# Dilated queries projected by seven-product block pairs together with the keys, rotated as stored halves; one weave of eight plain units over all twelve attention items

## The chip, the cores and the metric

The kernel runs on one core of a Trainium2 chip. The metric is device time in microseconds (us) of one execution; the comparison is between the median of runs of the kernel before and of the kernel after. The engines are named as in the profile: PE (matrix products), PEld (PE's weight loads), DVE, ACT and POOL (elementwise work), SP (a queue that here issues DMAs only).

## The reference

One block with three parallel mixers over 1024 tokens of width 1024, in float32. What matters here is the first mixer, the dilated window attention, and the merge gates:

```python
h = rms_norm(x, g_pre[layer])
a_qkv, bq, bk, bv, mq, ga, gb, gm, mg = jnp.split(h @ w_in[layer], split_at, axis=-1)
a_qkv = a_qkv.reshape(b, s, 3, n_groups * A_HEADS, HEAD_DIM)   # 3 groups x 8 heads x 64
aq = rope(a_qkv[:, :, 0], pos)
ak = rope(a_qkv[:, :, 1], pos)
av = a_qkv[:, :, 2]
for gi, (window, dil) in enumerate(A_GROUPS):                  # (128,1), (512,4), (2048,16)
    hs = slice(gi * A_HEADS, (gi + 1) * A_HEADS)
    o_g, lse_g = dilated_window_attention(aq[:, :, hs], ak[:, :, hs], av[:, :, hs], window, dil)
...
wts = jax.nn.softmax(jnp.stack(lses, axis=0), axis=0)          # over the three groups
oa = einsum(wts, outs)
...                                                            # grouped-query and memory attention
gates = sigmoid(mg + b_merge)                                  # 3 x 1024 columns of h @ w_in
merged = gates[0] * ya + gates[1] * yb + gates[2] * ym         # y: gated branch outputs, projected
x = x + rms_norm(merged @ w_out, g_post)
```

`rope` turns a head's first 32 features x1 and last 32 features x2 by an angle per token: x1 cos - x2 sin, and x1 sin + x2 cos.

## The kernel before

**Operands.** The normalised input is held transposed in SBUF, 8 tiles of 128 features by 1024 tokens, as a high part `hh` and a low part `hl` in a reduced format; weights are split likewise (`split`, L104: ACT copies the high part, DVE subtracts it from the source to get the low one). A product is three passes: high by high, high by low, low by high. A *unit* is 128 columns of `w_in` (1024 x 128 weights, 512 KB). A *plain* unit (`dense`, L139) takes 48 matmuls of 512 columns: 8 feature tiles, 3 passes, 2 token halves.

**Block products.** Two units can be made together by a scheme with seven products of half-sized blocks in place of eight (`PRODUCTS`: A11, A12, S2, S3, S4, S1, A22 of the weights, with sums S1 to S4 of weight blocks, against B and T blocks of the tokens, T being sums of token blocks that are kept in DRAM as `tsd`). Each product is 12 matmuls of 512 columns, a pair of units 84 instead of 96. The price is elementwise work per pair: four sums of weight blocks on POOL, splits of the blocks on ACT and DVE, and seven evacuations of PSUM with adds on DVE.

**Stages.** After the normalisation, the memory attention and the grouped-query attention come, in the order of time:

- the *value stage* (products for the dilated values);
- the *key stage* (loop at L1251): the twelve units of dilated keys as six pairs. `k_load` fetches two units, `k_sum` makes the sums on POOL, `k_own` and `k_block` split, `k_evac` takes PSUM, `k_out` adds the last part of a result and puts `turn_it` on the list `turns`: two multiplications on DVE, by the cosine table and by the sine table (`tab`, resident in SBUF), and two stores to `kd` issued from ACT's queue;
- the *weave* (from L1301 to the end of the pool `aa`): the twelve *items* of dilated attention, one for each pair of heads `p_` and group `g`, are interleaved with sixteen plain units: twelve of dilated queries (`add_a`), four of a mixer's gate (`add_ag`). `weave` (L176) places, in program order, a plain matmul or a piece of attention, whichever is behind by its planned cost. Deferred elementwise pieces lie in `pend`, and one is taken every third matmul. An item has 8 tiles of 128 queries: `scores` (PE), `soft` (a masked minimum on DVE, an exponential on ACT), `trans` (PE transposes, a copy by ACT), `pv` (PE), with `trans` three tiles behind `soft`. `combine` weighs the three groups of a head pair by their log-denominators, through DRAM, with multiplications on DVE (`weigh`, L1674) and adds on POOL;
- the *merge-gate stage* (loop at L1937): the other 22 of the 24 merge-gate units as eleven pairs of seven products, each finished by a tanh and a store to `thd`; two (`FILL_B`) are made earlier, beside the grouped-query attention;
- the branch products with the merge, and the output product.

**Queries and keys before.** A query unit's PSUM result is rotated by `q_rope`: four DVE operations of 32 partitions each for the crossed part (x2 by sine and x1 by sine, with the sign in the table), one DVE operation of 128 partitions for the straight part, and a POOL add that also writes the tokens sorted by residue class (`half_of`, `classes`). A key unit comes back from DRAM two items ahead: `k_fetch` loads `kraw` (cosine part) and, in four DMAs, `kswp` (sine part with the half heads exchanged), and `k_add` adds them on POOL, sorted by class. The first two query units and `first_keys` stand ahead of the first item, in a weave of their own; each later item has a weave of its own with one query unit, the last one the four gate units less one.

**Order.** In all these stages ACT, DVE, POOL and SP run in the order of the program (`manual_schedule`), and so does PE. An instruction that waits holds up everything behind it on its engine. Plain units of the weave: `add_au`, where `a_fetch` loads two units ahead and `a_split` splits the next unit's weights in two halves.

Of the kernel before, what the change touches and what calls it, by code (L numbers as in the profile page):

```python
# [16 lines left out]
NT = 8  # L17
# [33 lines left out]
def block(ctx: ExitStack, tc: tile.TileContext, x, xT, memT, cst, msk, bcst, tabA, gpost,  # L51
# [188 lines left out]
    kd = dram.tile([2, 12, P, S], F32, name="kd")  # L240
# [791 lines left out]
    def k_load(n, u):  # L1032

        KR[n, u] = wp.tile([P, 1024], F32, name="wr", bufs=WR)
        nc.sync.dma_start(KR[n, u], wu[4 * n + 2 * u + 1])


    AU = [2 * m for m in range(12)] + [U_G + 4 * i + p_ for i, p_ in GATES_A]
# [39 lines left out]
    kr_turn = iter(range(64))  # L1078

    def kr():  # L1080
        return vb.tile([P, 512], F32, name=("vy2", "vy3", "vv0", "vv1", "vy0", "vy1")[next(kr_turn) % 6])

    def k_out(n, u, t, ps_, z):

        r = kr()
        V.tensor_tensor(r, ps_, z, op=OP.add)

        def turn_it():
            c = kr()
            V.tensor_tensor(c, r, tab[0][:, half[t]], op=OP.mult)  # L1090
            V.tensor_tensor(r, r, tab[1][:, half[t]], op=OP.mult)
            for x, z in enumerate((c, r)):
                nc.scalar.dma_start(kd[x, 2 * n + u, :, half[t]], z)
        turns.append(turn_it)

    turns = []

    def k_evac(n, i, ps_):
        nm = PRODUCTS[i][0]
# [151 lines left out]
    for n in range(6):  # L1251
        for i, (an, bn) in enumerate(PRODUCTS):
# [11 lines left out]
            if i == 0:  # L1264
                k_block(n, "A22")
                if n < 5:
                    k_load(n + 1, 0)
            elif i == 1:
                k_block(n, "S4")
                if n < 5:  # L1270
# [6 lines left out]
            if n == 5:  # L1277
# [16 lines left out]
    close(kpp)  # L1294
    close(vbp)
# [7 lines left out]
    with tc.tile_pool(name="aa", bufs=1, reuse_waits="tile") as aa:  # L1303
# [7 lines left out]
        def half_of(ap, half, g):  # L1311

            if g == 0:
                return ap[:, half * 512:half * 512 + 512]
            n = S // DIL[g] // 2
            return ap.rearrange("p (r u) -> p r u", r=DIL[g])[:, :, half * n:half * n + n]

        def classes(ap, g):
            return ap if g == 0 else ap.rearrange("p (u r) -> p r u", r=DIL[g])

        OPS = {}

        def q_rope(o, half, p, g):

            t = slice(half * 512, half * 512 + 512)
            t1 = ab.tile([P, 512], F32, name="t1a", bufs=2)
            t2 = aa.tile([P, 512], F32, name="t2a", bufs=2)
            def cross(a):
                i, j = slice(32 * a, 32 * a + 32), slice(32 * (a ^ 1), 32 * (a ^ 1) + 32)
                V.scalar_tensor_tensor(t2[i], p[j], -0.125, tab[1][j, t], op0=OP.mult, op1=OP.mult)  # L1330

            def straight():
                V.scalar_tensor_tensor(t1, p, -0.125, tab[0][:, t], op0=OP.mult, op1=OP.mult)  # L1333
                G.tensor_tensor(half_of(o, half, g), classes(t1, g), classes(t2, g), op=OP.add)  # L1334

            pend.extend([lambda a=a: cross(a) for a in range(4)] + [straight])
# [21 lines left out]
        def add_a(p_, g):  # L1358
            d = OPS.setdefault((p_, g), {})

            def evac(half, p):
                if half == 0:
                    d["q"] = ab.tile([P, S], F32, name="aq", bufs=2)
                q_rope(d["q"], half, p, g)

            add_au(evac)

# [14 lines left out]
        KK = {}  # L1382

        def k_fetch(p_, g):

            KK[p_, g] = kr, ks = [ab.tile([P, S], F32, name=x) for x in ("kraw", "kswp")]
            nc.sync.dma_start(kr, kd[0, p_ * 3 + g])
            for a in range(4):
                i, j = slice(32 * a, 32 * a + 32), slice(32 * (a ^ 1), 32 * (a ^ 1) + 32)
                nc.sync.dma_start(ks[i], kd[1, p_ * 3 + g, j])  # L1390

        def k_add(p_, g):
            kr, ks = KK.pop((p_, g))
            ka = OPS.setdefault((p_, g), {})["k"] = ab.tile([P, S], F32, name="ak", bufs=2)
            for x in range(2):
                t = half[x]
                G.tensor_tensor(half_of(ka, x, g), classes(kr[:, t], g), classes(ks[:, t], g), op=OP.add)  # L1397

        def item(p_, g):
# [82 lines left out]
            def trans(T):  # L1482
# [25 lines left out]
                A.activation(pp[:, :k], tp[:, :k], AF.Copy)  # L1508
# [62 lines left out]
        def plan(it, pre, nxt):  # L1571
# [7 lines left out]
            def tokens(T):  # L1579
                if T >= 2:  # L1580
                    for nm, k in late[:2]:
                        split_block(nm, k)
                    del late[:2]
                if T == 5:
                    token_tiles("T1", [ab.tile([P, S], R, name=f"a{c}", bufs=2) for c in "qk"])
# [744 lines left out]
```

## Time and profile before

| what | value |
|---|---|
| median of 3 runs | 1414.22 us (1413.75 to 1416.55) |
| the profiled execution, first to last instruction (span) | 1412.1 us |
| mean granted TensorE clock | 0.999 |
| PE, DVE, ACT, POOL busy share of the span | 98%, 75%, 47%, 35% |
| key stage (580 to 692 us): PE, DVE, POOL busy | 112.0, 93.9, 32.3 us |
| weave (692 to 986 us): PE, DVE, ACT, POOL busy | 292.2, 207.4, 176.1, 108.2 us |
| merge-gate stage (986 to 1197 us): PE, DVE, POOL busy | 211.0, 171.5, 72.3 us |
| DMA | 216.01 MB, 153 GB/s over the span |

The busy time of an engine counts its instructions from start to end, with what they wait for inside an instruction. Matmuls overlap in the records, so their mean duration (some 400 ns for 512 columns) is longer than the distance of one from the next. In the lines quoted below, a timeline row is: start, duration, engine, line, operation, written tile <- read tiles, shape, count, and in brackets the idle time before it and what ended it. A group row is: line, engine, operation, tiles, shape, count | busy us, mean ns of one | idle us before it and what ended that. A row of a table by stage is: the stretch, its length, then busy us (and the number of instructions) of PE, PEld, DVE, ACT and POOL, the granted clock, DMA share and GB/s.

### The profile page before, as it was taken

The page shows a single profiled execution, that of the slowest core. Times are in us where ns is not written, and L with a number is a line of the kernel's source. Part 1 is how long each engine was busy: PE and PEld are TensorE (multiplying, and loading weights), DVE is VectorE, ACT ScalarE, POOL GpSimd, SP SyncE. Part 2 cuts the span into 40 slices and gives each one's busy share as a digit, 9 for nine tenths or more (in the row PEclk, how much of TensorE's full clock was granted, in tenths as well). Part 3 has the DMA queues.
Part 4 walks back from the last instruction along what each step waited for, and adds up shares of the span by engine and source line. Part 5 has one row for each costly group of instructions (what it writes and reads, how often), then busy time and mean ns, then how long its engine had stood idle before and what let it go on. Part 6 is the DMA issues. An engine that isn't in the chain of part 4 may idle for free.

```text
span 1412.1 us, 21576 instructions
## 1 busy us (share of the span) xinstructions
PE 1389.9 (98%) x7640; PEld 1126.2 (80%) x7640; DVE 1054.0 (75%) x1839; ACT 665.0 (47%) x1414; POOL 500.3 (35%) x390
## 2 busy tenths in 40 slices
PE   7999999999999999999999999999999999999997
PEld 7799986666666889888888878787888888888886
DVE  7768677767763688788875777765878788677977
ACT  6544365666555445222146666656443334222332
POOL 0416702666657000333153353520423331035303
PEclk9999999999999999999999999999999999999999
DMA  6356532322210787445643554555343543866255
GB/s 235 101 179 211 186 109 86 116 83 71 83 55 25 243 261 240 125 148 175 201 140 90 135 162 115 138 144 180 106 150 127 176 175 124 323 216 207 94 206 179
DMA packets 121852, 216.01 MB, mean 153 GB/s; under 512 B 25424, under 2 KB 58000, under 8 KB 121744
## 3 DMA queue, kind: packets, MB, share of 16 engines
q1 hardware_dynamic: 106096, 189.17, 42.0%
q10 hardware_dynamic: 15648, 25.47, 4.9%
q8 instruction: 60, 0.98, 0.3%
q14 instruction: 48, 0.39, 0.1%
HBM read 149.21 MB, written 65.37 MB: 152 GB/s over the span
## 4 chain that ended last, share of the span: by engine, by line
PE 88%; DVE 4%; ACT 3%; DMA 2%; POOL 2%; issue 1%; SPq 0%; DVEq 0%; ACTq 0%; POOLq 0%
PE s L125 23%; PE sc L125 9%; PE d L143 7%; PE d L147 6%; PE d L145 6%; PE s L1177 4%; PE s L2101 4%; PE ov L809 4%; PE s L1226 3%; PE tr L1522 3%; PE s L1466 3%; PE s L794 2%; PE s L793 2%; PE tr L775 2%; PE d L2101 2%; PE d L550 1%
## 5 line engine op out<-in xcount | busy, mean ns | idle before, releaser
L143 PE MATMUL d<-hh,wh 128*128 128x512 f32 x480 | 195.1, 406 | 2.4 <-DVE fth L228 2.4
L145 PE MATMUL d<-hl,wh 128*128 128x512 f32 x480 | 194.3, 405 | 0.0
L147 PE MATMUL d<-hh,wl 128*128 128x512 f32 x480 | 190.9, 398 | 0.0
L800 POOL TENSOR_TENSOR bl<-bl,bp 128x512 f32<-128x512 f32 x96 | 130.6, 1361 | 54.4 <-ACT bp L796 49.0
L105 ACT ACTIVATE wh<-wr 128x512 fp32r<-128x512 f32 (+1 forms) x93 | 72.5, 787 | 122.1 <-PE sc L125 75.3
L106 DVE TENSOR_TENSOR wl<-wr,wh 128x1024 fp32r<-128x1024 f32 (+1 forms) x67 | 85.3, 1285 | 50.2 <-ACT wh L105 50.2
L125 PE MATMUL sc<-hh,wh 128*128 128x512 f32 x384 | 118.5, 389 | 0.0
L143 PEld LDWEIGHTS d<-hh,wh 128*128 128x128 f32 x480 | 90.5, 188 | 27.8 <-issue 6.6
L147 PEld LDWEIGHTS d<-hh,wl 128*128 128x128 f32 x480 | 90.6, 189 | 21.0 <-issue 4.5
L1479 ACT ACTIVATE pra<-pra,sts 128x192 f32<-128x192 f32 (+2 forms) x192 | 84.3, 442 | 46.3 <-DVE sts L1478 45.8
L145 PEld LDWEIGHTS d<-hl,wh 128*128 128x128 f32 x480 | 90.6, 189 | 19.2 <-issue 4.5
L796 ACT ACTIVATE bp<-s 128x512 f32<-128x512 f32 x128 | 75.7, 595 | 43.3 <-PE s L794 42.3
L776 DVE TENSOR_REDUCE bn<-tr 128x1 f32<-128x512 f32 x128 | 84.9, 683 | 12.8 <-PE tr L775 11.7
L125 PEld LDWEIGHTS sc<-hh,wh 128*128 128x128 f32 x384 | 72.1, 188 | 14.9
L1330 DVE SCALAR_TENSOR_TENSOR t2a<-d,tab 32x512 f32<-32x512 f32 x96 | 65.9, 687 | 23.2 <-PE d L147 21.4
L2006 POOL TENSOR_TENSOR acc<-acc,th 128x1024 f32<-128x1024 f32 x15 | 41.4, 2757 | 109.1 <-DVE th L2005 109.1
L1789 POOL TENSOR_TENSOR sf<-wr 128x512 f32<-128x512 f32 x22 | 29.8, 1373 | 131.3 <-DVE ch L106 57.4
L125 PE MATMUL sc<-hl,wh 128*128 128x512 f32 x192 | 74.8, 389 | 0.0
L125 PE MATMUL s<-hh,ch 128*128 128x512 f32 x224 | 73.5, 390 | 0.0
L1334 POOL TENSOR_TENSOR aq<-t1a,t2a 128x512 f32<-128x512 f32 x24 | 44.6, 1861 | 72.0 <-DVE t1a L1333 72.0
L1819 ACT ACTIVATE rs<-rs,hbm 128x512 f32<-128x512 f32 x44 | 31.8, 722 | 76.5 <-DVE rs L1818 75.8
L1397 POOL TENSOR_TENSOR ak<-kraw,kswp 128x512 f32<-128x512 f32 x24 | 47.8, 2015 | 54.7 <-DMA std<-sr 21.2
(500 smaller groups left out, 3775.6 us busy)
## 6 DMA issues: line engine op xcount, KB each, us to landing
wr<-in_wu SPq DMA_DIRECT2D x64, 512.0 KB
th<-thd SPq DMA_DIRECT2D x24, 512.0 KB
thd<-rs ACTq DMA_DIRECT2D x44, 256.0 KB
kd<-vy ACTq DMA_DIRECT2D x32, 256.0 KB
g2d<-fth SPq DMA_DIRECT2D x24, 256.0 KB
wos<-os SPq DMA_DIRECT2D x12, 512.0 KB
kraw<-kd SPq DMA_DIRECT2D x12, 512.0 KB
kswp<-kd SPq DMA_DIRECT2D x48, 128.0 KB
```

The costliest lines, as they stand in the source:

```text
L105: A.activation(dst_h, src, AF.Copy)
L106: V.tensor_tensor(dst_l, src, dst_h.bitcast(F32), op=OP.subtract)
L125: PE.matmul(out_ps, a, b, start=i == 0, stop=i == n - 1)
L143: PE.matmul(dst, wh[:, k, :], hh[k][:, t], start=k == 0, stop=False)
L145: PE.matmul(dst, wh[:, k, :], hl[k][:, t], start=False, stop=False)
L147: PE.matmul(dst, wl[:, k, :], hh[k][:, t], start=False, stop=k == 7)
L776: fp["last"] = V.tensor_reduce(st[i]["n"][:, j, c:c + 1], s, axis=AX.X, op=OP.min)
L796: A.activation(pp, s, AF.Exp, scale=-1.0)
L800: G.tensor_tensor(lsum[i % 2], lsum[i % 2], pp, op=OP.add)
L1330: V.scalar_tensor_tensor(t2[i], p[j], -0.125, tab[1][j, t], op0=OP.mult, op1=OP.mult)
L1479: A.activation(src, src, AF.Exp, scale=-1.0, bias=bias, accum_out=sts[:, h, 1, T:T + 1])
L2101: PE.matmul(dst[:, e[0]:e[1]], a, b, start=k == 0 and q == 0, stop=k == 3 and q == 2)
```

## The change

- The twelve units of dilated queries go to the key stage. It now makes twelve pairs (`TURNS`: key pair, then query pair, for each half `c` of the heads and each group). A unit no longer holds two whole heads: it holds the first 32 features of four heads, and its partner the last 32, so that the two units of a pair are x1 and x2.
- `turn_it` still multiplies by both tables (for queries with the factor -0.125). When both units of a pair are there for a token half, POOL makes x1 cos - x2 sin and x1 sin + x2 cos and writes them by residue class into `ko` buffers. `k_store` puts them to `qkd` by eight DMAs of 32 partitions from SP's queue, one pair later.
- The order of the last products is changed (`KPROD`), the blocks A22 and S4 take buffers of the weight pool, and the places of the turns move by a slot.
- The weave holds eight plain units, four gate units as before and four merge-gate units (`FILL_A`), and is one weave over all items, with a pad of 7000 cost units ahead of the first scores and 1000 ahead of each of the last pieces. `qk_fetch` loads an item's rotated q and k two items ahead. `q_rope`, `k_fetch`, `k_add` are gone.
- In the weave, the copy of the transposed tiles goes from ACT to DVE, the low part of `a_split` and the weighing of the first three head pairs from DVE to POOL. The token blocks T2, T3, T1 are loaded and split from the eighth item on.
- The merge-gate stage makes nine pairs. Loads and products for the memory mixer's gated operand are spread over its later pairs (`PREP`).

```diff
+    KPROD = PRODUCTS[:4] + (PRODUCTS[6], PRODUCTS[4], PRODUCTS[5])
+    TURNS = [(j, c, g) for c in range(2) for g in range(3) for j in (1, 0)]
     def k_out(n, u, t, ps_, z):
         r = kr()
         V.tensor_tensor(r, ps_, z, op=OP.add)
+        j, c, g = TURNS[n]
         def turn_it():
-            c = kr()
-            V.tensor_tensor(c, r, tab[0][:, half[t]], op=OP.mult)
-            V.tensor_tensor(r, r, tab[1][:, half[t]], op=OP.mult)
-            for x, z in enumerate((c, r)):
-                nc.scalar.dma_start(kd[x, 2 * n + u, :, half[t]], z)
+            x = kr()
+            if j:
+                V.tensor_tensor(x, r, tab[0][:, half[t]], op=OP.mult)
+                V.tensor_tensor(r, r, tab[1][:, half[t]], op=OP.mult)
+            else:
+                V.scalar_tensor_tensor(x, r, -0.125, tab[0][:, half[t]], op0=OP.mult, op1=OP.mult)
+                V.scalar_tensor_tensor(r, r, -0.125, tab[1][:, half[t]], op0=OP.mult, op1=OP.mult)
+            RP[n, t, u] = x, r
+            if (n, t, 1 - u) in RP:
+                (ac, as_), (bc, bs) = [RP.pop((n, t, z)) for z in range(2)]
+                if n not in RO:
+                    RO[n] = [kp.tile([P, S], F32, name=f"ko{z}") for z in range(2)]
+                o1, o2 = RO[n]
+                G.tensor_tensor(half_of(o1, t, g), classes(ac, g), classes(bs, g), op=OP.subtract)
+                G.tensor_tensor(half_of(o2, t, g), classes(as_, g), classes(bc, g), op=OP.add)
         turns.append(turn_it)
+    def k_store(n):
+        j, c, g = TURNS[n]
+        for u, o in enumerate(RO.pop(n)):
+            for h in range(4):
+                a = h % 2 * 64 + 32 * u
+                nc.sync.dma_start(qkd[j, 2 * c + h // 2, g, a:a + 32], o[h * 32:h * 32 + 32])
...
     def a_split(n, x):
-        split(*[z[:, half[x]] for z in AW[n]], AR[n][:, half[x]])
+        h, l = [z[:, half[x]] for z in AW[n]]
+        A.activation(h, AR[n][:, half[x]], AF.Copy)
+        G.tensor_tensor(l, AR[n][:, half[x]], h.bitcast(F32), op=OP.subtract)
     def k_block(n, nm):
...
-             else kp.tile([P, 1024], R, name=f"ch{(n + (nm == 'S4')) % 2}"))
+             else wslot(int(nm == "A22")))
...
-    for n in range(6):
-        for i, (an, bn) in enumerate(PRODUCTS):
+    last = len(TURNS) - 1
+    for n in range(last + 1):
+        for i, (an, bn) in enumerate(KPROD):
...
-            if i in ((1, 2, 4, 6) if n else (4, 6)) and turns:
+            if i in ((1, 2, 3, 6) if n else (3, 6)):
                 turns.pop(0)()
+            if i == 4 and n:
+                k_store(n - 1)
...
     while turns:
         turns.pop(0)()
+    k_store(last)
...
-                A.activation(pp[:, :k], tp[:, :k], AF.Copy)
+                V.tensor_copy(pp[:, :k], tp[:, :k])
...
             def weigh(g):
-                V.tensor_tensor(ogv, ogv, wv, op=OP.mult)
+                (G if p_ < 3 else V).tensor_tensor(ogv, ogv, wv, op=OP.mult)
...
+        def qk_fetch(p_, g):
+            d = OPS[p_, g] = {}
+            for j, x in enumerate("qk"):
+                d[x] = ab.tile([P, S], F32, name="a" + x, bufs=2)
+                nc.sync.dma_start(d[x], qkd[j, p_, g])
...
+        def first():
+            qk_fetch(*seq[0])
             items[0]["values"][0][0]()
+            qk_fetch(*seq[1])
+            yield FIRST_PAD
+        def every():
+            yield from first()
+            for n in range(len(seq)):
+                yield from run(plan(items[n], items[n - 1] if n else None, items[n + 1]))
+            for fn, cost in plan(None, items[-2], None):
+                yield cost + LAST_PAD
+                fn()
+        weave(len(AU), every(), FIRST_PAD + 12 * (NT * (SOFT + 100.0) + 2 * JOINED + 100.0) + 5 * LAST_PAD)
...
+FILL_A = (18, 19, 20, 21)
+FIRST_PAD, LAST_PAD = 7000.0, 1000.0
```

More of the change, by code (lines that the diff above doesn't have):

```diff
@@ L1309, in block @@
         G.memset(vpart, 0.0)
[L1311 to L1319, printed above, removed]
-        OPS = {}
[L1323 to L1336, printed above, removed]
+        OPS = {}
         def add_au(evac):
@@ L1380, in add_ag, with add_am, evac @@
             add_au(evac)
[L1382 to L1397, printed above, removed]
+        def add_am(j):
+            spilled.add(j)
+            def evac(h, p):
+                th = aa.tile([P, 512], F32, name="fth", bufs=2)
+                def first():
+                    V.tensor_tensor(th, p, rb[:, half[h]], op=OP.mult)
+                    A.activation(th, th, AF.Tanh, scale=0.5, bias=hbm[:, j:j + 1])
+                pend.extend([first, lambda: nc.sync.dma_start(thd[j, :, half[h]], th)])
+            add_au(evac)
+        def qk_fetch(p_, g):
[3 more added lines that the diff above has]
+                nc.sync.dma_start(d[x], qkd[j, p_, g])
         def item(p_, g):
@@ L1618, in plan @@
                         out.append(it["values"][1])
+                    if it and it["ahead"]:
+                        out.append((lambda: qk_fetch(*it["ahead"]), 0.0))
                     if pre and it:
@@ L1715, in split_block @@
             split(h, l, l.bitcast(F32))
-        late = []
         todo = []
@@ L1880, in block @@
     COM = {(0, 0): 0, (1, 4): 1, (1, 6): 2, (2, 1): 3, (3, 1): 4, (3, 2): 5, (4, 1): 6, (4, 2): 7, (5, 1): 8, (5, 6): 9}
+    PREP = {}
+    for k in range(4):
+        for fn, at in ((g_load, 0), (g_mult, 4)):
+            at += k * 7 * (last - 6) // 4
+            PREP.setdefault((6 + at // 7, at % 7), []).append((fn, k))
     def slot(n, i):
@@ L1910, in slot @@
             pre["pp"], pre["p"] = pool("pre", "right")
-        k = n - (last - 4)
-        if 0 <= k < 4:
-            if i == 0:
-                g_load(2, k)
-            elif i == 4:
-                g_mult(2, k)
+        if n >= 6 and (n, i) in PREP:
+            for fn, k in PREP[n, i]:
+                fn(2, k)
         if n == last:
@@ L2238, in layout @@
     units = []
-    for p in range(4):
+    first = (np.arange(4)[:, None] * 64 + np.arange(32)[None]).reshape(-1)
+    for q in range(2):
         for g in range(3):
-            b = (g * 8 + 2 * p) * 64
-            units += [unit(1536 * j + b + np.arange(128)) for j in range(2)]
+            for j in (1, 0):
+                for u in range(2):
+                    units.append(unit(1536 * j + (g * 8 + 4 * q) * 64 + 32 * u + first))
     for i in range(3):
```

106 lines of the change are left out of this document (43 added, 63 removed).

## The prediction, made before the changed kernel was run

> **What bounds the kernel now.** I read the page first: the span, the engines' shares and the chain that ended last.
>
> ```profile
> span 1412.1 us, 21576 instructions
> PE 1389.9 (98%) x7640; PEld 1126.2 (80%) x7640; DVE 1054.0 (75%) x1839; ACT 665.0 (47%) x1414; POOL 500.3 (35%) x390
> PE 88%; DVE 4%; ACT 3%; DMA 2%; POOL 2%; issue 1%; SPq 0%; DVEq 0%; ACTq 0%; POOLq 0%
> ```
>
> PE is the bound: busy 98% of the span and 88% of the chain. A change pays only by the PE work that it takes away, and costs wherever it makes PE wait. The second view is busy time by stage, with bounds at the three stages that the change touches: the key stage, the weave, the merge-gate stage.
>
> ```profile
> core 0: us, PE busy (x) PEld busy (x) DVE busy (x) ACT busy (x) POOL busy (x), PEclk, DMA share, GB/s
> 580.00:692.00 112.00, 112.00 (x492) 92.27 (x491) 93.87 (x120) 27.47 (x45) 32.26 (x20) 1.00 0.48 161
> 692.00:986.00 294.00, 292.23 (x2158) 238.00 (x2156) 207.43 (x601) 176.07 (x562) 108.21 (x56) 1.00 0.51 144
> 986.00:1197.00 211.00, 211.00 (x943) 174.73 (x943) 171.47 (x217) 89.32 (x138) 72.31 (x45) 1.00 0.42 140
> ```
>
> PE never waits in the first and third, and hardly in the second. The key stage gives the price of one 512-column matmul: 112.00/492 = 0.2276 us. In that stage DVE is busy 84% and POOL 29%: whoever adds to these two comes near a limit that the PE share hides.
>
> The third view is the order of time on DVE and POOL within one key pair.
>
> ```profile
> 646.75 2.20 DVE L106 TENSOR_TENSOR wl<-wr,wh 128x1024 fp32r<-128x1024 f32 x1 [0.25 <-ACT wh L105]
> 648.87 0.68 DVE L1110 TENSOR_TENSOR vv<-s,vv 128x512 f32<-128x512 f32 x1
> 649.47 1.18 DVE L106 TENSOR_TENSOR vS<-vgt,vS 128x512 fp32r<-128x512 f32 x1
> 650.57 1.78 DVE L1090 TENSOR_TENSOR vy<-vy,tab 128x512 f32<-128x512 f32 x1
> 652.39 0.69 DVE L1091 TENSOR_TENSOR vy<-vy,tab 128x512 f32<-128x512 f32 x1
> ```
>
> ```profile
> 646.58 1.29 POOL L1058 TENSOR_TENSOR vot<-wr 128x512 f32<-128x512 f32 x1 [0.63 <-DVE vS L106]
> 647.94 2.16 POOL L1058 TENSOR_TENSOR vot<-vot,wr 128x512 f32<-128x512 f32 x1
> 650.18 1.62 POOL L1058 TENSOR_TENSOR vrt<-wr,vot 128x512 f32<-128x512 f32 x1
> ```
>
> Here is what my forecast rests on. The two engines take turns. A DVE operation with both inputs in SBUF does not run beside a POOL operation: the split at 646.75 ends 1.08 us after POOL's first sum has ended (647.87), the multiply at 650.57 ends 0.55 us after POOL's third (651.80), though alone it takes 0.69. POOL waits likewise: its sum at 647.94 ends 1.15 us after the split's end (648.95), and takes 1.29 alone. Each hand-over saves about 0.14. The DVE add at 648.87, whose input lies in PSUM, runs its 0.68 beside POOL and pays nothing. So I split DVE's work in locked operations (two SBUF inputs) and free ones (PSUM input).
>
> **Removed PE work.** Key stage 6 pairs of 84 matmuls become 12: 504 to 1008. Weave 16 units of 48 become 8: 768 to 384. Merge gates 11 pairs become 9: 924 to 756. In sum 2196 to 2148, so 48 x 0.2276 = **-10.9 us**. The attention matmuls (292.23 - 768 x 0.2276 = 117.4 us of the weave) stay. The new weave is 384 x 0.2276 + 117.4 = 205 us of PE work.
>
> **Key stage, twelve pairs: what DVE and POOL carry.** DVE's list per pair is as before: seven adds from PSUM (free), one split of 1024, five splits of 512, eight multiplies (locked; for queries a scalar_tensor_tensor). POOL has its four sums, and now four rotating adds or subtracts with it (two per token half), which were POOL work of the weave. Their price is in the weave's rows: the same shape, read by residue class.
>
> ```profile
> 727.03 4.11 POOL L1397 TENSOR_TENSOR ak<-kraw,kswp 128x512 f32<-128x512 f32 x2 [2.83 <-DMA kswp<-kd]
> 731.11 2.06 POOL L1334 TENSOR_TENSOR aq<-t1a,t2a 128x512 f32<-128x512 f32 x1
> 748.31 2.54 POOL L1397 TENSOR_TENSOR ak<-kraw,kswp 128x512 f32<-128x512 f32 x2 [6.51 <-PE s L1466]
> 751.01 1.29 POOL L1334 TENSOR_TENSOR aq<-t1a,t2a 128x512 f32<-128x512 f32 x1 [0.16 <-DVE t1a L1333]
> ```
>
> ```profile
> 732.15 2.16 DVE L106 TENSOR_TENSOR wl<-wr,wh 128x512 fp32r<-128x512 f32 x2 [2.47 <-ACT wh L105]
> 1119.72 2.31 DVE L1857 SCALAR_TENSOR_TENSOR ot<-ot,gt 128x1024 f32<-128x1024 f32 x1
> 1119.32 1.62 POOL L1789 TENSOR_TENSOR sf<-wr,sf 128x512 f32<-128x512 f32 x1
> ```
>
> Items with dilation 1 cost 1.29 (748.31, 751.01), those with 4 or 16 cost 2.06 (727.03, 731.11). The last three rows show that turns hold for these kinds too: two splits that start at 732.15 end 1.14 us after the strided operation's end (733.17), and a scalar_tensor_tensor ends 1.09 us after POOL's (1120.94).
>
> PE needs 84 x 0.2276 = 19.1 us a pair. I lay DVE and POOL out in the diff's order. From the turn of the first token half (seventh slot) to that of the second (third slot of the next pair): first rotation 2.06, the S2 split that stands behind it 0.55, second rotation 1.92 with two evacuations beside it, A22 split 0.55, S4 split 0.6, two multiplies 1.2 (their buffer comes free after the second rotation), an evacuation 0.6, two multiplies 1.2: 8.7 us. From there back to the first half's turn: rotation 2.06, S1 split 0.55, rotation 1.92, the 1024 split 1.08, then three sums of 1.15 and two multiplies and a split of 0.55 in turns, the fourth sum 1.15 with the evacuations beside it, two multiplies 1.2: 5.61 + 5.10 + 1.15 + 1.2 = 13.1 us. The loop is 21.8 us. With dilation 1 it is 4 x 0.77 = 3.1 less, 18.7, and PE's 19.1 decides. Eight pairs of twelve have dilation 4 or 16: 8 x 2.7 = **+21.6 us**. From below: if all free work hides, the locked sum 4 x 1.15 + 4 x 1.92 + 13 x 0.55 + 1.08 = 20.5 remains, +11. From above: with the 4.2 us of free adds half uncovered it would be 24 a pair, and dilation 1 at 20.5: +45. I take the layout, since everything in it has a row. Who waits: PE's third product of a pair needs the S2 split, its fifth and sixth the A22 and S4 splits, all of them now behind a rotation; PE runs some products ahead and then falls back to the loop's pace.
>
> [...]
>
> The stores move from ACT's queue to SP's, eight of 128 KB a pair for eight of 256 KB. SP waits in `k_store` for the rotations, and behind it stands the next pair's `k_load`, due a pair later: nothing, by that distance; if the stores are late, POOL's next rotation waits for the `ko` buffers, which the upper bound holds. The other block order and the blocks' new buffers change only which slot reads them.
>
> **The start of the weave.** Before, 96 plain matmuls lay ahead of the first scores. Now the pad is 7000 of an attention cost of 126000, so 384 x 7/126 = 21, some 22 with the first piece: 5.0 us.
>
> ```profile
> 691.34 1.29 DVE L1086 TENSOR_TENSOR vy<-s,vv 128x512 f32<-128x512 f32 x2 [2.04 <-PE s L125]
> 697.72 0.69 DVE L1091 TENSOR_TENSOR vv<-vv,tab 128x512 f32<-128x512 f32 x1
> 709.62 1.75 SPq L1390 DMA_DIRECT2D kswp<-kd  x4
> 715.71 2.13 POOL L1397 TENSOR_TENSOR ak<-kraw,kswp 128x512 f32<-128x512 f32 x1 [5.31 <-DMA kswp<-kd]
> ```
>
> DVE's tail after the last key product (691.3) ends at 698.4: 7.1 us. Behind it now come two rotations (4.1), eight store issues on SP at 1.75/4 (3.5), and only then, behind them on SP, the first item's q and k, 4.3 us from the last issue (711.37) to the reader's start (715.71) plus 0.4 of issue. 7.1 + 4.1 + 3.5 + 4.7 = 19.4, less 5.0 of cover: PE waits **+14.4 us**. If a short tail takes 9 off, 5; if the `ak` buffer waits for the stores to land, 18.
>
> **The weave itself.** Per tile PE has 205/96 = 2.1 us.
>
> ```profile
> L1330 DVE SCALAR_TENSOR_TENSOR t2a<-d,tab 32x512 f32<-32x512 f32 x96 | 65.9, 687 | 23.2 <-PE d L147 21.4
> L1333 DVE SCALAR_TENSOR_TENSOR t1a<-d,tab 128x512 f32<-128x512 f32 x24 | 16.5, 687 | 0.1
> L106 DVE TENSOR_TENSOR wl<-wr,wh 128x512 fp32r<-128x512 f32 x32 | 27.3, 875 | 25.7 <-ACT wh L105 25.6
> L1677 DVE TENSOR_TENSOR og<-og,wgt 128x1024 f32<-128x1024 f32 x9 | 19.1, 2118 | 3.8 <-DMA wgt<-wgd 3.8
> L1508 ACT ACTIVATE app<-tr 128x384 f32<-128x384 f32 x40 | 19.2, 480 | 11.6 <-PE tr L1496 10.8
> L1508 ACT ACTIVATE app<-tr 128x512 f32<-128x512 f32 x24 | 14.3, 595 | 16.2 <-PE tr L1505 16.1
> L1508 ACT ACTIVATE app<-tr 128x256 f32<-128x256 f32 x32 | 12.2, 381 | 6.6 <-PE tr L1505 6.4
> L1334 POOL TENSOR_TENSOR aq<-t1a,t2a 128x512 f32<-128x512 f32 x24 | 44.6, 1861 | 72.0 <-DVE t1a L1333 72.0
> L1397 POOL TENSOR_TENSOR ak<-kraw,kswp 128x512 f32<-128x512 f32 x24 | 47.8, 2015 | 54.7 <-DMA std<-sr 21.2
> ```
>
> DVE loses 65.9 + 16.5 + 27.3 + 19.1 and gains the 96 copies of transposed tiles, between ACT's 45.7 and 96 x 0.68 = 65 (I take 55), and 8 x 0.68 for four merge units: 207.4 - 128.8 + 55 + 5.5 = 139 of 205. ACT: 176 - 45.7 and less. POOL: 108.2 - 92.4 + 16 x 1.29 + 9 weighings at twice 2.06 = 74. None is a bound. A weighing of 4.1 us can hold up a token split on DVE and with it the next tile: once at full length, **+4 us**; 0 to 12. The merge stage keeps its list per pair, under 211.00 us of PE in 211: nothing for the earlier `g_load`, nothing for the smaller number of pairs beyond what is counted.
>
> **Sum.** Span 1412.1 - 10.9 + 21.6 + 14.4 + 4 = 1441.2. The median of the runs, 1414.22, lies 2.1 above the span: **1443.3 us**.
>
> **Rivals.** *PE stays fed* (0.14): locked operations find gaps, the start wait halves or goes; 1403.3 to 1411. For it: all three stages run at PE's pace now, with DVE at 84% in the first. Against it: the turns in the rows above; it holds if the pair's loop of DVE and POOL stays under 19.1 us. *Only the start waits* (0.08): 1412.1 - 10.9 + 14.4 + 2.1 = 1417.7, half of it within the measurement. *The thin weave does not hide the softmax* (0.10): with half the plain matmuls per tile, scores of a half item wait for the softmax's last two tiles; at one DVE lag of 1.5 us in each of 24 halves +36, 1479. Against it: DVE has 139 of 205 us. That the change does less than it says is excluded: the counts of matmuls are in the loops.
>
> **How the numbers follow.** My case has 0.68. Low bounds of all terms give 1412.1 - 10.9 + 11 + 5 + 2.1 = 1419, high ones 1412.1 - 10.9 + 45 + 18 + 12 + 2.1 = 1478. The range, 1412 to 1480, leaves out most of the first rival and some above. Faster by over 0.2% (some 3 us, about what runs can tell): 0.14. Within: 0.04, half of the second rival. Slower: 0.68 + 0.10 + 0.04 = 0.82.
>
> **What would show it.** Right: key stage of 245 to 255 us with PE busy near 90%, locked DVE operations of 1.2 to 2.5 us, POOL busy over half of it, period 22 us for dilation 4 and 16 and 19 for 1; a gap of over 5 us on PE ahead of the first scores; weave 205 to 225, merge stage 172. Wrong: key stage at 229 with PE full, or first scores without a wait (faster), or weave of over 230 us with waits at scores (the last rival).

## The result, and the profile after

The change makes the kernel slower: 1468.55 us (median of 4 runs, 1467.77 to 1471.60) against 1414.47 us in runs of the kernel before on the same chip; ratio 1.0381, 95% interval 1.0366 to 1.0396. The forecast was 1443.3 us, range 1412 to 1480. Profiled execution: 1468.73 us, span 1467.0.

From the page after, the span, the engines and the chain; PE's share fell from 98% to 95%.

```profile
span 1467.0 us, 21487 instructions
PE 1399.1 (95%) x7592; PEld 1123.6 (77%) x7592; DVE 1074.4 (73%) x1874; ACT 633.9 (43%) x1330; POOL 592.5 (40%) x431
...
PE 24%; DVE 1%; ACT 1%; issue 1%; DMA 0%; POOL 0%; ACTq 0%; DVEq 0%; POOLq 0%
```

The chain adds up to under 30% here and shows no cause. Busy time by stage does; the bounds are the first matmuls of key stage, weave, merge-gate stage and branch products.

```profile
core 0: us, PE busy (x) PEld busy (x) DVE busy (x) ACT busy (x) POOL busy (x), PEclk, DMA share, GB/s
580.32:839.45 259.13, 242.60 (x1011) 193.75 (x1010) 217.00 (x244) 52.65 (x86) 172.96 (x89) 0.97 0.33 96
839.45:1077.79 238.34, 208.89 (x1782) 166.95 (x1780) 135.17 (x549) 135.00 (x460) 70.92 (x37) 0.95 0.56 169
1077.79:1249.37 171.58, 171.58 (x759) 141.92 (x757) 139.18 (x176) 73.04 (x114) 59.19 (x37) 1.00 0.45 149
```

The kernel before, by the same bounds (the prediction's windows are rounder):

```profile
578.79:693.93 115.14, 115.14 (x507) 94.80 (x506) 97.01 (x125) 27.77 (x46) 33.22 (x21) 1.00 0.48 160
693.93:987.09 293.16, 291.38 (x2165) 237.31 (x2164) 206.19 (x598) 176.07 (x562) 107.25 (x55) 1.00 0.52 145
987.09:1196.70 209.61, 209.61 (x926) 173.62 (x925) 170.69 (x215) 89.32 (x138) 72.31 (x45) 1.00 0.42 141
```

The merge stage is at PE's pace and its 171.6 us are as worked out. The losses lie in the first two. PE's waits by what ended them (total, times, longest), first for the key stage, then for the weave:

```profile
PE s L125 <- DVE vS L106: 16.4, 9, 2.3
```

```profile
PE s L1473 <- DMA ak<-qkd: 20.0, 1, 20.0
PE tr L1529 <- DVE app L1515: 3.8, 3, 2.2
PE tr L1512 <- ACT og L1537: 1.5, 1, 1.5
PE tr L1512 <- ACT sr L1547: 1.1, 2, 0.8
```

In the key stage PE waits for splits on DVE. In the weave it waits once, 20 us, for the first item's keys, and 9.4 us in small waits at transposes and value products.

One turn of a dilated pair, in order of time (start, duration; in brackets the idle time before and its releaser), DVE first and POOL beside it:

```profile
688.78 0.69 DVE L1102 TENSOR_TENSOR vy<-s,vv 128x512 f32<-128x512 f32 x1
692.67 0.69 DVE L1102 TENSOR_TENSOR vy<-s,vv 128x512 f32<-128x512 f32 x1 [3.20 <-POOL ko L1120]
...
694.60 0.69 DVE L106 TENSOR_TENSOR wh<-vrt,wh 128x512 fp32r<-128x512 f32 x1 [0.65 <-ACT wh L105]
...
697.86 0.69 DVE L1109 TENSOR_TENSOR vy<-vy,tab 128x512 f32<-128x512 f32 x1
698.46 0.68 DVE L1144 TENSOR_TENSOR vv<-s,vv 128x512 f32<-128x512 f32 x1
699.06 1.96 DVE L106 TENSOR_TENSOR vS<-vot,vS 128x512 fp32r<-128x512 f32 x1
700.94 3.09 DVE L106 TENSOR_TENSOR wl<-wr,wh 128x1024 fp32r<-128x1024 f32 x1
703.96 1.78 DVE L1111 SCALAR_TENSOR_TENSOR vy<-vv,tab 128x512 f32<-128x512 f32 x1
```

```profile
690.64 1.99 POOL L1120 TENSOR_TENSOR ko<-vy,vy 128x512 f32<-128x512 f32 x1
697.90 2.57 POOL L1119 TENSOR_TENSOR ko<-vy,vy 128x512 f32<-128x512 f32 x1 [5.26 <-DVE vy L1108]
700.43 2.52 POOL L1120 TENSOR_TENSOR ko<-vy,vv 128x512 f32<-128x512 f32 x1
702.91 2.27 POOL L1060 TENSOR_TENSOR vgt<-wr 128x512 f32<-128x512 f32 x1
```

The locked operations take what the forecast laid out: split 1.96, long split 3.09, multiply 1.78. The second row is new: an evacuation from PSUM, of the kind that takes 0.68 us beside POOL's rotation (698.46), waits 3.20 us, because the ring of six buffers gives it the buffer that POOL's second rotation (ends 692.63) is still reading. PE waits too, and behind its wait of 2.28 us here the granted clock fell. Three stretches of this pair, with PEclk as the third column from the right:

```profile
679.50:688.70 9.20, 7.09 (x30) 4.95 (x28) 9.13 (x10) 1.79 (x3) 7.59 (x6) 1.00 0.34 89
688.70:692.10 3.40, 3.18 (x8) 2.50 (x9) 0.77 (x2) 0.00 (x0) 3.40 (x2) 0.50 0.27 104
692.10:701.10 9.00, 9.00 (x40) 7.33 (x39) 7.72 (x11) 2.58 (x4) 3.73 (x3) 1.00 0.18 59
```

PE waited 2.28 us up to 688.92, and the granted clock is 0.50 for 3.4 us: 8 matmuls, where at 0.2276 us each there would be 15. Five such stretches stand in the key stage, one behind each of its five 2.28 to 2.30 us waits; its waits of 1.85 us and less have none. Experiment 6 shows that this slows the matmuls there, but does not make the stage longer.

The start of the weave: DVE's last turns, the last rotations, the stores, the loads, the first scores.

```profile
848.10 0.69 DVE L1102 TENSOR_TENSOR vv<-s,vv 128x512 f32<-128x512 f32 x1 [3.39 <-POOL ko L1120]
...
850.76 0.69 DVE L1112 SCALAR_TENSOR_TENSOR vv<-vv,tab 128x512 f32<-128x512 f32 x1
...
853.16 1.88 POOL L1120 TENSOR_TENSOR ko<-vv,vy 128x512 f32<-128x512 f32 x1
853.23 3.58 SPq L1128 DMA_DIRECT2D qkd<-ko  x8
...
857.85 0.42 SPq L1404 DMA_DIRECT2D ak<-qkd  x1
...
865.39 1.01 PE L1473 MATMUL s<-ak,aq 64*128 64x128 f32 x5 [20.03 <-DMA ak<-qkd]
```

It is the predicted chain, with the same buffer wait (3.39 us) in its first link.

### The profile page after: what moved, and what is told of

Same layout as the page of the kernel before. It is cut to its first block, busy times and chain, and to the rows that moved or that the text cites. A ratio compares the mean times of both kernels' runs of the same rounds, so it can differ in the third digit from the quotient of the medians.

```text
span 1467.0 us, 21487 instructions
## 1 busy us (share of the span) xinstructions
PE 1399.1 (95%) x7592; PEld 1123.6 (77%) x7592; DVE 1074.4 (73%) x1874; ACT 633.9 (43%) x1330; POOL 592.5 (40%) x431
## 5 line engine op out<-in xcount | busy, mean ns | idle before, releaser
L143 PE MATMUL d<-hh,wh 128*128 128x512 f32 x352 | 144.0, 409 | 2.5 <-DVE fth L228 2.5
L147 PE MATMUL d<-hh,wl 128*128 128x512 f32 x352 | 144.2, 410 | 0.3 <-POOL wl L1050 0.2
L145 PE MATMUL d<-hl,wh 128*128 128x512 f32 x352 | 143.0, 406 | 0.0
L105 ACT ACTIVATE wh<-wr 128x1024 fp32r<-128x1024 f32 (+1 forms) x65 | 57.3, 884 | 104.0 <-PE sc L125 75.2
L1515 DVE COPY app<-tr 128x384 f32<-128x384 f32 (+2 forms) x96 | 52.2, 545 | 66.0 <-PE tr L1512 37.9
L125 PE MATMUL s<-hh,wh 128*128 128x512 f32 x264 | 97.5, 391 | 0.0
L776 DVE TENSOR_REDUCE bn<-tr 128x1 f32<-128x512 f32 x128 | 84.9, 684 | 12.6 <-PE tr L775 11.4
L106 DVE TENSOR_TENSOR wl<-wr,wh 128x1024 fp32r<-128x1024 f32 x39 | 70.1, 1799 | 23.0 <-ACT wh L105 23.0
L125 PE MATMUL s<-hl,wh 128*128 128x512 f32 x216 | 84.3, 390 | 0.0
L143 PEld LDWEIGHTS d<-hh,wh 128*128 128x128 f32 x352 | 67.0, 190 | 20.2 <-issue 6.5
L125 PE MATMUL s<-kT,vS 128*128 128x512 f32 x216 | 62.9, 437 | 13.9 <-DVE vS L106 13.9
L1485 DVE CUSTOM_DVE_ANT_0 pra<-s,mask 128x192 f32<-128x192 f32 (+2 forms) x192 | 59.0, 345 | 16.0 <-PE s L1473 16.0
```

Of the source, the lines that this page charges most:

```text
L105: A.activation(dst_h, src, AF.Copy)
L106: V.tensor_tensor(dst_l, src, dst_h.bitcast(F32), op=OP.subtract)
L125: PE.matmul(out_ps, a, b, start=i == 0, stop=i == n - 1)
L143: PE.matmul(dst, wh[:, k, :], hh[k][:, t], start=k == 0, stop=False)
L145: PE.matmul(dst, wh[:, k, :], hl[k][:, t], start=False, stop=False)
L147: PE.matmul(dst, wl[:, k, :], hh[k][:, t], start=False, stop=k == 7)
```

## The experiments

All kernels start from the kernel after. Stage lengths run from first matmul to first matmul. My theory after the result: the key stage's loss is the lock between DVE's two-operand reads and POOL, with the ring's wait and the half clock on top (the half clock dropped out with experiment 6); the weave's is the start plus a softmax chain that too little plain work covers.

**1. The ring's wait.** Each of the eight results of a pair gets a fixed place in the six buffers, so that the second evacuation takes one that is free.

```diff
-name=(...)[next(kr_turn) % 6]
+name=(...)[(8 * n + k) % 6]     # k by quarter: sums 0, 2, 4, 5; second results 1, 3, 6, 7
```

> The changed kernel with the six rotation buffers given out by role instead of by turn: the last evacuation of a pair then takes a buffer whose reader is long done, and no longer waits for POOL's second rotation (an idle of DVE of 3.2 us a pair in the changed kernel, 32.7 us in all). Theory A (POOL's rotations shut out DVE's operations with two SBUF inputs, and the buffer wait only adds to it): the loop of a pair with dilation 4 or 16 falls from 23.4-23.9 us to about 21.9, the key stage from 259 to 240-248 us, the half-clock stretches in it go with the shorter PE waits; 1450 us, within 1445 to 1457. Rival B (the buffer wait is the whole loss, the turns cost nothing that PE sees): key stage 230 us, 1438 us.

Measured 1453.62 us, ratio 1.0271 (1.0256 to 1.0286): 14.9 us gained, as theory A had it. The key stage took 245.2, PE's waits in it fell from 16.5 to 7.8 us (three half-clock stretches stayed, where A expected none). From a pair's first rotation to the next pair's a steady loop is 21.8 to 22.3 us with dilation 4 and 16, in place of 23.4 to 23.9, and 18.9 with dilation 1, in place of 20.5. So the buffer order costs about half of the key stage's excess over PE's 230.3, and the lock remains.

**2. Rotations that read densely.** POOL reads and writes without the sorting by class, at 1.29 us each; the attention then runs over unsorted tokens.

```diff
-G.tensor_tensor(half_of(o1, t, g), classes(ac, g), classes(bs, g), ...)
+G.tensor_tensor(half_of(o1, t, 0), classes(ac, 0), classes(bs, 0), ...)
```

> The changed kernel whose rotations leave out the sorting by residue class: the same four POOL operations a pair, all of them contiguous (the dilated groups 4 and 16 then attend over unsorted tokens). Theory A: each rotation holds POOL 1.29 instead of 2.06 us, so all pairs behave as those of dilation 1 do now; loop at most 20.4 us, key stage 230 to 240 us, 1439 to 1450 us. Rival C (DVE and POOL have too many instructions, whatever their length, or the waits are those of buffers and queues): the loop keeps its 23.4 us, 1466 to 1470 us.

Measured 1444.42 us, 1.0203 (1.0186 to 1.0220). Key stage 238.1, its pairs 19.2 us up to the sixth and then 20.45, one wait of about 1 us per pair and no half clock. With POOL's shorter hold the stage is 21.0 us shorter, as the lock says. But the ring's wait gets shorter with it (1.83 us a pair, in place of up to 3.55), so this run doesn't tell the two apart.

**3. Rotations on DVE.** POOL keeps its four sums; DVE carries 4 operations more per pair.

```diff
-G.tensor_tensor(half_of(o1, t, g), ...)
+V.tensor_tensor(half_of(o1, t, g), ...)
```

> The changed kernel with the four rotating adds of a pair on DVE instead of POOL. Theory A: DVE's own work rises by 4 x 0.69 = 2.8 to some 16 us a pair, under PE's 19.1, and only POOL's four sums (1.15 each) still shut it out: loop 19.2 to 20.5 us, key stage 231 to 245 us, 1440 to 1455 us. Rival C (DVE is simply full: it was busy 84% of the key stage before): more work on DVE makes the loop longer than 24 us, 1480 us or more.

Measured 1449.57 us, 1.0245 (1.0230 to 1.0261): DVE with the rotations' work on top is faster than with the rotations on POOL, which rules out C. Key stage 245.4, pairs from the fifth on of 20.2 to 21.2 us and one of 23.4. The ring's wait is gone here too, so this run doesn't tell it from the lock either.

**4. More plain work ahead of the first scores.**

```diff
-FIRST_PAD, LAST_PAD = 7000.0, 1000.0
+FIRST_PAD, LAST_PAD = 28000.0, 1000.0
```

> The changed kernel with the pad ahead of the first scores raised from 7000 to 28000: 73 plain matmuls instead of 22 lie ahead of them, 11.6 us more of cover, and the items get 3.2 instead of 3.8 plain matmuls a tile. If the first scores' wait (20.0 us) is a plain exposed latency: it falls to 8-9 us, the rest stays, 1457 us (1453 to 1460). Rival (the weave is thin, its items need all plain matmuls to hide the softmax): the waits between the items grow from some 9 us by as much as is won, 1464 to 1472 us.

Measured 1465.81 us, 1.0364 (1.0345 to 1.0384), not told from the kernel after, as the rival had it. The first scores came without a wait, at 865.36, the same time as before; from there to the end of the weave it took 211.0 us instead of 212.4, though 51 plain matmuls (11.6 us) were no longer in that stretch. The plain matmuls ahead of the scores waited 5.6 us themselves, and in the items what was moved ahead was given back as waits:

```profile
PE tr L1529 <- DVE app L1515: 6.9, 4, 3.1
PE tr L1503 <- DVE app L1515: 3.3, 6, 0.9
```

**5. The lock by itself.** Three of the four quarters of a pair keep their sum in the PSUM bank, so six of eight multiplies read PSUM and one table. Counts and sizes of the operations stay.

```diff
-        r = kr()
+        r = kr() if (u, t) == (1, 1) else ps_
         V.tensor_tensor(r, ps_, z, op=OP.add)
...
-                V.tensor_tensor(r, r, tab[1][:, half[t]], op=OP.mult)
+                V.tensor_tensor(s, r, tab[1][:, half[t]], op=OP.mult)     # s = kr() where r is ps_
```

> Three of the four quarters of a product pair keep their sum in the PSUM bank, so that 6 of the 8 multiplies of the turn read PSUM and one SBUF table instead of two SBUF operands; counts of operations, POOL's rotations and PE's work stay. Theory A (VectorE's two-operand reads of SBUF and POOL's rotations exclude one another): the sums that read PSUM take 0.685 us beside the rotations already now, so the six multiplies fall to about 0.7 us each; the dilated pairs go from 23.8 to 19.2-20, the key stage from 259 to 228-238, no half clock in it: 1436 to 1448 us. Rival B (only the ring of six buffers holds VectorE up): this kernel can gain no more than separate buffers by role did (1453.6): 1452 to 1458. Rival C (VectorE's and POOL's plain amount of work): nothing moves, 1466 to 1471.

Measured 1433.38 us, 1.0124 (1.0109 to 1.0139): 35 us gained, 2.6 below the end of theory A's range. Its two stages:

```profile
579.77:810.11 230.34, 230.34 (x1011) 189.50 (x1010) 204.40 (x249) 53.70 (x86) 162.13 (x91) 1.00 0.39 112
810.11:1040.72 230.61, 208.54 (x1781) 167.01 (x1779) 131.97 (x543) 134.98 (x460) 68.14 (x35) 0.96 0.57 170
```

The key stage is at PE's floor, 230.34 us for 1008 matmuls, with POOL still busy 162 us in it. Two groups of multiplies, out of PSUM and out of SBUF:

```profile
L1110 DVE TENSOR_TENSOR vy<-s,tab 128x512 f32<-128x512 f32 x12 | 8.1, 676 | 0.0
...
L1113 DVE SCALAR_TENSOR_TENSOR vv<-vv,tab 128x512 f32<-128x512 f32 x2 | 3.1, 1574 | 0.1
```

With the first operand in PSUM a multiply took 0.676 us in the mean of 12, and the two of the row below, their operands both in SBUF, 1.574; four others of that line with both in SBUF took 0.692. This change also moves buffers, so the ring's wait went with the lock; experiments 1 and 5 together say that about 14 us are the ring's order and 15 the lock's. The first scores' wait fell to 12.8 us, because DVE's tail shortened with it.

**6. The copies of transposed tiles back on ACT.**

```diff
-V.tensor_copy(pp[:, :k], tp[:, :k])
+A.activation(pp[:, :k], tp[:, :k], AF.Copy)
```

> The copies of the transposed probabilities go back from VectorE to ScalarE (96 of them, 0.56 us in the mean on VectorE, about 0.49 on ScalarE in the kernel before). Theory A (between items TensorE waits for copies queued behind VectorE's softmax and splits): the waits between items fall from 9.4 to 2-4 us: 1459 to 1465 us. Rival B (ScalarE's exponentials are as late as the copies; ScalarE's busy time goes from 135 to about 182 of 212 us): no gain or a loss, 1467 to 1476. Either way the key stage stays at 259.

Measured 1466.25 us, 1.0357 (1.0342 to 1.0373): its interval overlaps that of the kernel after, so no gain that these runs tell. The weave is 4.3 us shorter (234.0) and its small waits fall from 9.4 to 7.0, but the stages behind it took 4.3 us more in this execution. The time lies between the two theories' ranges and decides nothing.

The run settles another thing, since it leaves the key stage as it was. The stage, and PE's waits in it:

```profile
579.57:838.57 259.00, 240.25 (x1011) 191.39 (x1010) 216.64 (x243) 52.65 (x86) 172.80 (x89) 0.98 0.33 96
PE s L125 <- DVE vS L106: 18.7, 11, 2.3
```

Three half-clock stretches stand in it, not five, PE waits 18.7 us instead of 16.4, and the length is 259.0, as in the kernel after (259.1). Experiments 4, 7 and 8, with six, four and four stretches, took 259.2, 259.3 and 259.2. So DVE and POOL set the pace of this stage. PE's half clock did not lengthen it: with fewer such stretches PE only waited more.

**7. The last stores on POOL's queue.**

```diff
-nc.sync.dma_start(qkd[j, 2 * c + h // 2, g, a:a + 32], ...)
+(nc.gpsimd if n == last else nc.sync).dma_start(qkd[...], ...)
```

> The eight stores of the last pair are issued from POOL's queue instead of SP's. Theory A (the first scores wait because SP issues their q and k, stored long before, behind the last pair's stores): SP reaches the loads when the mask's buffer is free, the wait before the first scores falls from 20 to 8-14 us: 1455 to 1463 us. Rival B (the loads' own buffers are those the last turns still use, and SP's order costs its eight issues only): 16 to 17 us of wait remain, 1464 to 1467. Rival C (POOL's queue is late for its own work after that): no gain, 1467 to 1472.

Measured 1470.06 us, 1.0385 (1.0367 to 1.0402): no gain, wait 19.9 us. The first item's q and k were stored over 215 us earlier, but SP's loads of them wait for the memory that they go to:

```profile
SPq L1404 <- DMA qkd<-ko: 8.5, 2, 7.6
SPq L1404 <- DVE vy L1111: 7.9, 1, 7.9
```

The `aq` load waits for the last turn's buffer, the `ak` load for the last stores to have read `ko`. Theory A falls; B named the mechanism but expected 3 to 4 us from the queue, and there were none. C's range holds the time. On POOL the stores start only behind its second rotation and their issues end 4.1 us after it, on SP 1.8 us; whether that ate up B's gain was not tried.

**8. The weighing back on DVE.**

```diff
-(G if p_ < 3 else V).tensor_tensor(ogv, ogv, wv, op=OP.mult)
+V.tensor_tensor(ogv, ogv, wv, op=OP.mult)
```

> The nine weighings of the first three head pairs go back from POOL to VectorE. Theory A (a weighing on POOL, 2.9 us, holds VectorE's splits and exclusive reads up): a small gain of the waits between items, 1463 to 1467 us. Rival B (VectorE's 19 us more in 212 make copies and softmax later): 1469 to 1476. No change, 1467 to 1469, would say that neither is near the path.

Measured 1470.27 us, 1.0385 (1.0369 to 1.0400): not told from the kernel after, though the time lies at the low end of B's range. DVE's busy time in the items rose from 127 to 145 us with it, and in this execution they took 2.4 us longer. So 18 us more on DVE cost at most that: its time is not what the items lack most.

**9 to 11. The parts together.** With the sums in PSUM, copies on ACT and a lead of 30000 (9); the same with the copies on DVE (11); the first with 3000 kept back per step behind the last item (10).

```diff
-FIRST_PAD, LAST_PAD = 7000.0, 1000.0
+FIRST_PAD, LAST_PAD = 30000.0, 1000.0     # 10: 30000.0, 3000.0
```

> Sums left in PSUM for the turns, copies of the transposed probabilities on ScalarE, and the lead of the plain units ahead of the first scores raised from 7000 to 30000. Theory A (three separate losses: the key stage's lock, the wait before the first scores, the copies between items): key stage 230, no wait over 3 us before the first scores, 4 to 9 us of waits between items, so the weave takes 211 to 217 instead of 230.6: 1412 to 1420 us. Rival B (the items take about 211 us whatever plain work lies among them, as with the lead alone): weave 225 to 230, 1427 to 1433.

> The same without the copies' move: sums in PSUM and the lead of 30000, copies on VectorE. Theory A (copies on VectorE set the items' floor of 211 us once plain work is taken out of them): weave 224 to 230, 1425 to 1432 us. Rival B (the floor is elsewhere, or was an effect of VectorE's late key-stage tail): within 3 us of the kernel with the copies on ScalarE, whatever that takes.

> As the first of these, with the plain work kept for each step behind the last item raised from 1000 to 3000. Theory A (the 4.7 us of waits behind the last item are for want of plain work there): 2 to 4 us under the first of these. Rival B (the plain work taken out of the middle opens as much there): within 1 us of it, or above.

Measured 1426.78 (1.0080, 1.0066 to 1.0095), 1430.44 (1.0110, 1.0096 to 1.0124) and 1422.75 us (1.0057, 1.0043 to 1.0070). The start wait is gone in 9 and 11 (0.14 and 0.20 us) and 1.1 in 10, yet the weaves took 225.4, 228.5 and 222.3 us, with 15.8, 17.3 and 12.3 us of waits. For 9 its theory A was too hopeful by 7 us: more waits opened between items (B). Copies on ACT are worth 3.7 us (9 against 11, which lies in its A's range and 0.7 us outside B's), the work kept for the end another 4.0 (10 against 9), as its theory A had it. How the copies matter shows in what ACT's exponentials and DVE's copies or minima wait for, in the stretch of the items (after the bar: busy us, mean ns; after the next: idle us before them, and what ended it); first 11, then 9:

```profile
L1487 ACT ACTIVATE pra<-pra,sts 128x192 f32<-128x192 f32 (+2 forms) x192 | 84.5, 441 | 57.2 <-DVE sts L1486 55.9 <-PE tr L1530 0.2
L1516 DVE COPY app<-tr 128x384 f32<-128x384 f32 (+2 forms) x96 | 52.2, 544 | 63.7 <-PE tr L1513 36.9 <-PE tr L1504 25.9
```

```profile
L1487 ACT ACTIVATE pra<-pra,sts 128x192 f32<-128x192 f32 (+2 forms) x192 | 84.1, 441 | 7.6 <-DVE sts L1486 7.6
L1486 DVE CUSTOM_DVE_ANT_0 pra<-s,mask 128x192 f32<-128x192 f32 (+2 forms) x192 | 56.9, 348 | 70.4 <-PE s L1474 63.0 <-ACT og L1538 4.4 <-PE tr L1504 1.1
```

On DVE a copy waits 64 us in all for PE's transposes, and the minima behind it in the queue wait with it, so ACT waits 57 us for minima. On ACT the copies let DVE's minima run ahead, and ACT waits 7.6.

**12. Copies by turns.** Sums in PSUM; copies of odd tiles on DVE, of even ones on ACT, the statistics' copies on DVE, lead 31000, a little plain work more at the first item and the end (3500).

```diff
+if T % 2:
+    V.tensor_copy(pp[:, :k], tp[:, :k])
+else:
+    A.activation(pp[:, :k], tp[:, :k], AF.Copy)
```

> Sums in PSUM; the copies of the transposed probabilities by turns on VectorE (odd tiles) and ScalarE (even ones); the 12 small copies of the statistics on VectorE; plain work kept back a little more for the first item (400 for each of its first nine steps, lead 31000) and the end (3500). Theory A (the waits between items are for copies queued behind one engine's softmax work): of the 12.3 us of waits left in the weave with a lead of 30000 and 3000 at the end, 5 to 8 remain, 1416 to 1419 us, no faster than the kernel before (1415). Rival B (the plain work taken for both ends opens as much in the middle): 1421 to 1425 us. To beat the kernel before by 0.2% it would have to come under 1412, with 2 us of waits in the weave or less.

Measured 1433.97 us, 1.0131 (1.0114 to 1.0148): worse than either theory, 11 us above experiment 10. The waits in the weave grew to 22.8 us. DVE holds only half of the copies, and waits longer ahead of them:

```profile
L1517 DVE COPY app<-tr 128x384 f32<-128x384 f32 (+2 forms) x48 | 26.1, 544 | 77.6 <-PE tr L1513 44.2 <-PE tr L1504 33.1
L1487 ACT ACTIVATE pra<-pra,sts 128x192 f32<-128x192 f32 (+2 forms) x192 | 84.3, 441 | 45.4 <-DVE sts L1486 45.2
```

So in the items a share of busy time says little. That what stands behind a waiting copy decides fits these rows, but is not shown by this run alone: it also moves the statistics' copies (7.0 us of PE's waits end on them) and the lead, and these were not run apart. No version beat the kernel before; the best, experiment 10, is 0.57% slower.

## Why the prediction was right in sign and short in size

The forecast case held, all its terms have the right sign, and three are too small. The total is 25.3 us short: 7.2 in the key stage, 5.6 at the start, 9.3 in the items, the other 3.2 in small things (the key stage began 1.5 us later, the last stages took 2.2 more, the span lies 0.5 nearer to the median). Of the signs named for it, the gap ahead of the first scores, POOL's share and the merge stage came as told. The key stage (259.1, not 245 to 255) and the weave (238.3, not 205 to 225) did not, and the weave is over the 230 that was named as a sign of the last rival; 20.0 of it are the start.

- **Removed PE work, -10.9: right.** At PE's pace the three stages would be 230.34 (experiment 5), 205 and 171.58, 606.9 in sum, 11.0 under the 617.9 before.
- **Key stage, +21.6: it took 28.8** (259.1 less 230.3). Of the laid-out loop the part from the second half's turn on took 13.1 us, as told; the first part 10.3 against 8.7 (turns ending at 688.26, 698.55 and 711.66). The step that failed is the evacuation in that part, which I put beside the second rotation at no cost: it waits 3.20 us for the ring's buffer and comes behind it. ACT's copies stand behind the same evacuation, so a split then waits 0.65 us for ACT. I had seen this kind of wait for the multiplies of the pair ("their buffer comes free after the second rotation"), not for the sum. The loop took 23.4 to 23.9 us (22 forecast), and 20.5 with dilation 1, where I had PE's 19.1 decide: near the 24 and 20.5 of my upper bound. Without the ring's wait (experiment 1) it is as laid out, 21.8 to 22.3 and 18.9. That the term is only 7.2 short is luck: the layout by itself gave 14.9 in that run, 6.7 less than my sum, since DVE and POOL may end the stage behind PE and the last pair has no sums of a next one, and the ring added 13.9. PE busy was 242.6 of 259.1, 94%, DVE 84%, POOL 67%.
- **The 0.14 saved at a hand-over: it held in the row above.** The split at 699.06 ends 0.55 us after POOL's rotation (700.47), where the one at 694.60, with no POOL operation beside it, takes 0.69. Experiment 1, without the ring's wait, has an excess of 14.9 us, below even my layout (the first dilated pairs took 19.2 us on PE, out of its lead, which I had not taken off).
- **Start, +14.4: it took 20.0.** The chain was the right one. From the last key product to the first scores it is 25.9 us, where I had 19.4, less 5.9 of plain work (5.0). DVE's tail took 12.0 instead of 7.1, 3.4 of it the ring's wait, and the 7.1 was too long for the kernel before: I counted it from the sixth product's end (691.3), while the last one ends where the weave begins (693.93), which leaves 4.5. q and k landed 7.5 us after their issue instead of 4.7. In experiment 5, without that wait, the chain is 18.2. The bounds of 5 to 18 did not hold it, since the upper one had no price for a longer tail.
- **Items, +4: 13.3** (238.3 less 205 less 20.0), 9.4 of it waits and the rest PE at a granted clock of 0.50 (7.6 us of it behind the first scores' wait and near the end, so 3.8 lost). I looked for a weighing that holds a split up; experiment 8 moved it and gained nothing. The copies were counted as busy time, 55 us (52.2 measured) of an engine with room. What I didn't ask is what stands behind a copy while it waits for PE. Experiment 9 against 11 gives 3.7 us for it, and 6 points the same way; what the rest of the waits hangs on stays open.
- **The rivals.** *PE stays fed* was held out by what I named, the loop over 19.1 us; experiment 5 shows that six operands moved to PSUM get there; fewer were not tried. *The thin weave does not hide the softmax* has some truth: with the start wait taken away (4, 9, 11) the items still take over 205 us, and in 11 all but 2 of the 12.6 us of start wait that the padding took away (against experiment 5) came back, some 8 as waits and the rest as slower matmuls. Its price of 36 was far too high.

## What to carry to other kernels

Before work moves to POOL, list DVE's operations with two SBUF inputs; see whether a result can stay in PSUM until its last reader (in experiment 5 multiplies that read it there took 0.676 us, two with both operands in SBUF 1.574, four 0.692). When the order of a ring's users changes, follow each buffer through a full turn, evacuations too: a rotating index hid a 3.2 us wait here that cost about 14 us in all. On an in-order queue, ask of each instruction that waits for PE what is behind it; in experiment 11 DVE was busy 125.9 of the items' 209.9 us, 60%, and ACT's exponentials waited 55.9 us for it.

## What the runs showed of the hardware that was not expected

In the key stage of the kernel after, each of the five waits of 2.28 to 2.30 us was followed by 3.4 us at a granted clock of 0.50 (above), though PE was full up to the next wait (21.12 of 21.12 us from 688.92 on). Behind the waits of 1.85, 1.31 and 1.25 us there the clock stayed at 1.00. In experiment 1 one of 1.94 us was followed by the half clock, and in experiments 6, 7 and 8 some of 2.28 us were not, so the length alone doesn't settle it. Two stretches of experiment 6, each behind a wait of 2.28 us:

```profile
712.93:716.34 3.41, 3.41 (x10) 2.63 (x9) 0.91 (x2) 0.13 (x1) 2.46 (x2) 0.50 0.00 0
736.82:740.23 3.41, 3.41 (x17) 2.82 (x16) 2.14 (x4) 2.00 (x4) 0.60 (x1) 1.00 0.13 25
```

PE made 10 matmuls in the first, at 0.50, and 17 in the second, at 1.00. What tells the two apart was not shown, nor how it is in other kernels. In the key stage of the kernel after, the half clock cost no time (experiment 6).
